# Layer 1 of a two-layer trunk with a routed mixture of experts: another row order for the experts' input weights, and another instruction order on GpSimd

## The chip, the cores and the metric

The kernel runs on one core of a Trainium2 chip. The metric is the device time of one execution in microseconds (us). The kernel before took 2328.43 us (median of 3 runs, 2326.62 to 2334.72). The execution that the profiler recorded took 2327.7 us, and its span, from the first to the last instruction, is 2326.0 us.

The engines are called as in the profile: PE is TensorE (PEld its weight loads), DVE is VectorE, ACT is ScalarE, POOL is GpSimd, SP is SyncE. SP issues nearly all plain loads and stores. POOL issues all indirect transfers (gathers and scatters).

## The reference

Two layers over 1024 tokens of width 1024, float32. Each layer is a mixer (layer 0 a causal pooling mixer, layer 1 gated linear attention, "GLA") and then a mixture of 64 experts, of which every token uses two:

```
for i in range(2):
    shift1, scale1, gate1, shift2, scale2, gate2 = split(silu(c) @ w_mod[i] + b_mod[i], 6)
    h = rmsnorm(x, norm_gain[i, 0]) * (1 + scale1) + shift1
    x = x + gate1 * (pool_mixer(h) if i == 0 else gla_mixer(h))
    h = rmsnorm(x, norm_gain[i, 1]) * (1 + scale2) + shift2
    x = x + gate2 * hier_moe(h)          # group top-1, then two experts of that group
return rmsnorm(x, final_norm_g)

# one expert, over the tokens t routed to it:
gate, up = split(t @ w_in[i, e], 2)      # w_in[i, e] is 1024 x 768
y = (silu(gate) * up) @ w_out[i, e]      # w_out[i, e] is 384 x 1024
```

Each expert's weights are 3 MB (w_in) and 1.5 MB (w_out), read once for each layer whatever the number of its tokens.

## The kernel before

**Weights.** SBUF is divided into 16 slots of [128 partitions, 3072 floats], 1.5 MB each. One expert takes three of them, called thirds: thirds 0 and 1 are the two halves of w_in, third 2 is w_out. `third_load` (L495) issues one 1.5 MB DMA on SP's queue for each. For a half of w_in partition p gets the four rows k*128 + p of that half, which lie apart in memory, 3,072 bytes each. For w_out partition p gets the three rows 3p to 3p+2, 12,288 bytes that lie side by side. In layer 1 the thirds go round a ring of 14 slots (`RING1`), so that loads run up to 14 thirds ahead, and `queued` (L488) makes each load wait until the load three before it has landed (`DEEP` = 3). SP works strictly in order.

**Tokens.** The normalised rows (without scale and shift) lie in HBM as `h_d`. For each expert POOL gathers 64 token rows, as two halves of 512 channels on 128 partitions, into a buffer `XG` (`gather`, L501). `expert_in` (L508) transposes it on PE in four pieces of 128 channels (L512), and applies scale and shift per channel while it moves the pieces from PSUM to SBUF, on ACT (L520) and DVE (L522). The columns of scale and shift are `modA[:, l, 1]` and `sec(l, 3)`, one column of 128 partitions for each block of 128 channels.

**An expert.** `expert_first` multiplies by w_in (L538, 32 matmul instructions on PE), `expert_hidden` makes silu(gate)*up (L545 on ACT, L546 on DVE), `expert_turn` transposes it (L554 on PE, L555 on ACT), `expert_last` multiplies by w_out (L563), and `expert_add` scales the result on DVE (L568) and has POOL add it to the rows of `x_d` by an indirect DMA with accumulation (L569, here called the scatter). One such sequence is called a pass. An expert with more than 64 tokens takes a second pass with the same weights (`expert_either`). Layer 1 has 68 passes for 64 experts. While PE is busy with one expert, the transposes of the next one stand behind its first product (L512 after L538), so that ACT and DVE work beside PE. Each scatter waits until the one before it has landed, since both may add to the same rows.

**Order on POOL in layer 1's mixture.** `moe` (L608) walks over the experts. In the program's text the step of expert e is: `gather` of expert e+4 (L647; `AHEAD1` = 4, eight buffers in `MAIN1`), then `ahead(e + 3)` (a test of the count on L619 and L630, with a gather of the second 64 tokens in it if there are more than 64), then the scatter or scatters of expert e. Four gathers and three tests stand before the loop. The stage is built under

```
    with tc.manual_schedule(engines={ET.PE}):
        moe(1, RING1, MAIN1, (4, 5, 10, 11), load1, AHEAD1, 3)
```

so that PE keeps the program's order, while the scheduler of the framework places the instructions of the other engines, POOL among them. The load of the fourteenth third of the ring has a dependency written by hand on the fourth gather (L1396).

**Before that mixture** the GLA stage of layer 1 runs over 8 tiles of 128 tokens. Its queries, keys, values, gates and residual rows are fetched by indirect gathers on POOL, two tiles ahead (L1138, L1142, L1146, L1147), and in the middle of it the last columns of the modulation are made (`late_mod`, `mod_scale`).

Of the kernel before, what the change touches and what calls it, by code (L numbers as in the profile page):

```python
# [7 lines left out]
F32 = mybir.dt.float32  # L8
# [6 lines left out]
ET = mybir.EngineType  # L15
# [21 lines left out]
def trunk_kernel(ctx, tc, x_in, c_in, norm_gain, w_mod, b_mod, pool_w, pool_b, pool_scale,  # L37
# [4 lines left out]
    V, S, T, G, SP = nc.vector, nc.scalar, nc.tensor, nc.gpsimd, nc.sync  # L42
# [4 lines left out]
    dram = ctx.enter_context(tc.tile_pool(name="dram", bufs=1, space=bass.MemoryType.DRAM))  # L47

    A = [slots.tile([128, 3072], F32, name=f"slot{i}") for i in range(16)]
# [3 lines left out]
    v_d = dram.tile([SEQ, 1024], F32, name="v_d")  # L53
    r_d = dram.tile([SEQ, 1024], F32, name="r_d")
    z_d = dram.tile([SEQ, 16], F32, name="z_d")

    def part(slot, kb, n):
        a = int(kb * 256)
        return A[slot][:, a:a + n]

    def ps():
        return psum.tile([128, 512], F32, name="ps")
# [10 lines left out]
    ident = cv(128)  # L73
# [6 lines left out]
    modA = cv(32).rearrange("p (a b c) -> p a b c", a=2, b=2)  # L80
# [21 lines left out]
    XG = [XGt[:, i, :] for i in range(4)] + [part(15, 7 + 2 * i, 512) for i in range(2)] \  # L102
# [93 lines left out]
    def mod_scale(l, s):  # L196
        V.scalar_tensor_tensor(modA[:, l, s, :], mod[:, l, 24 * s + 8:24 * s + 16], 1.0,
                               C1[:, 96 + (2 * l + s) * 8:96 + (2 * l + s) * 8 + 8], op0=OP.add, op1=OP.mult)

    def sec(l, s):  # L200
        return mod[:, l, 8 * s:8 * s + 8]

    def row(col, half, diag):
        d = diag.rearrange("p (a b) -> p a b", a=4)
# [273 lines left out]
    hv = h_d.rearrange("t (g d) -> (t g) d", g=2)  # L478
    yv = [y.rearrange("t (g d) -> (t g) d", g=2) for y in x_d]

    def expert_load(win, wout, sl):
        behind.clear()
        for j in range(3):
            third_load(win, wout, j, sl)

    behind = []

    def queued(ins):  # L488

        if len(behind) >= DEEP:  # L490
            tc.add_manual_dep(ins.ins, behind[-DEEP].name, DATA_SYNC, reason="loads leave room for gathers")
        behind.append(ins.ins)
        return ins

    def third_load(win, wout, j, sl):  # L495
        if j < 2:
            src = win.rearrange("(k p) f -> p k f", p=128)
            return [queued(SP.dma_start(A[sl[j]].rearrange("p (k f) -> p k f", k=4), src[:, 4 * j:4 * j + 4]))]
        return [queued(SP.dma_start(A[sl[2]], wout.rearrange("(p c) d -> p (c d)", c=3)))]
# [8 lines left out]
    def expert_in(l, i, g, first=None):  # L508
        xT = part(15, 2 * i, 512).rearrange("p (c g t) -> p c g t", c=4, g=2)
        pp = [ps(), ps()]  # L510
        for cc in range(4):
            T.transpose(pp[cc % 2][:, cc // 2 * 128:cc // 2 * 128 + 128], XG[g][:, cc * 128:(cc + 1) * 128], ident)  # L512
        with tc.issue_after(first()) if first else ExitStack():
            for cc in range(4):
                pv = pp[cc % 2][:, cc // 2 * 128:cc // 2 * 128 + 128].rearrange("p (g t) -> p g t", g=2)
                for g in range(2):
                    kc = 4 * g + cc
                    sc, sh = modA[:, l, 1, kc:kc + 1], sec(l, 3)[:, kc:kc + 1]
                    if cc % 2:
                        S.activation(xT[:, cc, g, :], pv[:, g, :], AF.Identity, bias=sh, scale=sc)  # L520
                    else:
                        ins = V.tensor_scalar(xT[:, cc, g, :], pv[:, g, :], sc, sh, op0=OP.mult, op1=OP.add).ins  # L522
        return ins
# [146 lines left out]
    def rest(l, lo, hi, flag, src, sl, bufs):  # L670

        bi, bg = bufs
        base, en = ov[:, 0:1], ov[:, 1:2]
        pb, R, w = ov[:, 2:10], ov[:, 10:34], ov[:, 34:35]
        Rv = R.rearrange("p (t w) -> p t w", w=3)
        Sl = A[sl[0]][:, 0:512]
        nmax = nc.values_load(flag, min_val=0, max_val=SEQ, skip_runtime_bounds_check_because=COUNT_REASON)
        with tc.If(nmax > 128):
            V.memset(en, float(lo))
            with tc.For_i(lo, hi, 1) as e:  # L680
                n = nc.values_load(cnt_i[0:1, bass.ds(e, 1)], min_val=0, max_val=SEQ,
                                   skip_runtime_bounds_check_because=COUNT_REASON)
                with tc.If(n > 128):
                    V.memset(base, 128.0)
                    with tc.For_i(128, n, 64):
                        p = ps()
                        m = 0
                        for k in range(2):
                            V.tensor_scalar(pb, pos(k), base, None, op0=OP.subtract)
                            slots_of(Sl, pb, 0)  # L690
                            V.tensor_scalar(pb, eid(k), en, None, op0=OP.is_equal)
                            for c, a in enumerate((tokno, place, wk(k))):
                                V.tensor_tensor(Rv[:, :, c], pb, a, op=OP.mult)
                            for t in range(NT):
                                for g in range(2):
                                    T.matmul(p[64 * g:64 * g + 64, 0:3], Sl[:, t * 64:(t + 1) * 64], Rv[:, t, :],
                                             start=m == 0, stop=m == 15)
                                m += 1
                        V.tensor_scalar(ovi, p[:, 0:2], 2.0, gcol, op0=OP.mult, op1=OP.add)
                        V.tensor_copy(w, p[:, 2:3])  # L700
                        gather(ovi[:, 0:1], bg)
                        expert_in(l, bi, bg)
                        expert_load(*src(e), sl)
                        expert_out(l, bi, sl, (w, ovi[:, 1:2]), bg)
                        V.tensor_scalar(base, base, 64.0, None, op0=OP.add)
                V.tensor_scalar(en, en, 1.0, None, op0=OP.add)
# [129 lines left out]
    def load0(e, j, sl):  # L836
        r = e // 8
        if r not in regs:
            regs[r] = nc.values_load(cnt_i[0:1, NE + 16 + r:NE + 17 + r], engines=(ET.SP,), min_val=0, max_val=56,
                                     skip_runtime_bounds_check_because="eight times the number of a group")  # L840
        d = bass.ds(regs[r] + e % 8, 1)
        third_load(moe_w_in[0, d].rearrange("o k f -> (o k) f"), moe_w_out[0, d].rearrange("o k f -> (o k) f"), j, sl)

    for s in range(3):
        load0(0, s, RING0[0:3])
# [452 lines left out]
    pulled = [gl_load2(0), gl_load2(1)]  # L1298

    def load1(e, j, sl):  # L1300
        return third_load(moe_w_in[1, e], moe_w_out[1, e], j, sl)

    def fill1(lo, hi):
        for s in range(lo, hi):
# [20 lines left out]
    with tc.manual_schedule(engines={ET.PE}):  # L1325
        for t in range(NT + 2):
# [17 lines left out]
                columns.pop(0)()  # L1344
            if t == 2:
                mod_scale(1, 1)
            if t > 1:
                route_turn(t - 2, 1, xnb, hTb)
            if t > NT:
# [46 lines left out]
    tc.add_manual_dep(load1(4, 1, RING1[12:14] * 2)[0].ins, ins.name, DATA_SYNC,  # L1396
                      reason="what is needed sooner goes first")
    G.memset(part(15, 7, 1024), 0.0)
    with tc.manual_schedule(engines={ET.PE}):
        moe(1, RING1, MAIN1, (4, 5, 10, 11), load1, AHEAD1, 3)  # L1400
    rest(1, 0, NE, cnt_i[0:1, NE + 8:NE + 9],
         lambda e: tuple(w[1, bass.ds(e, 1)].rearrange("o k f -> (o k) f") for w in (moe_w_in, moe_w_out)),
# [44 lines left out]
```

## Time and profile before

| | |
|---|---|
| median of 3 runs | 2328.43 us |
| profiled execution | 2327.7 us |
| its span | 2326.0 us |
| PE busy | 1984.6 us (85%) |
| DVE, ACT, POOL busy | 718.9, 622.7, 496.9 us |
| bytes moved by DMA | 770.03 MB, mean 331 GB/s |
| layer 1's mixture, from expert 0's first matmul to the last one | 1495 to 2295 us of the span |

The page gives busy time per engine, then the span in 40 equal slices of 58 us. A digit is the busy share in tenths. The row DMA is the mean busy share of the 16 DMA engines. For a single stage, the views by window, the waits and the timeline within that stage are of more use than the page.

### The profile page before, as it was taken

How to read it: one execution, taken by the hardware profiler on the slowest of the kernel's cores; microseconds unless marked ns; L12 is line 12 of the kernel's file. 1: busy time of each engine (PE TensorE's matmuls, PEld its weight loads, DVE VectorE, ACT ScalarE, POOL GpSimd, SP SyncE). 2: the span in 40 equal slices, each digit the busy share in tenths (PEclk: the TensorE clock that was granted, in tenths of full speed). 3: DMA queues.
4: the chain of work that ended last, by engine and by line, in shares of the span. 5: the costliest groups of instructions: out<-in, count | busy, mean ns of one | idle time of the engine just before them, and what ended most of it. 6: DMA issues, size and time to landing. Idle time of an engine off the chain costs nothing. (4 is left out here: it accounts for less than half of the span.)

```text
span 2326.0 us, 31279 instructions
## 1 busy us (share of the span) xinstructions
PE 1984.6 (85%) x11195; PEld 945.5 (41%) x11196; DVE 718.9 (31%) x1759; ACT 622.7 (27%) x1418; POOL 496.9 (21%) x422
## 2 busy tenths in 40 slices
PE   7968888899999999999888999888878777778784
PEld 5644333344444444444334565433323332333331
DVE  3454545211121121212147567422211111112122
ACT  4222323322222121212126665221211111112113
POOL 0303222122222221222124110222212212122210
PEclk9979999999999999999988999899999999999997
DMA  9979989998978999989945942699999999999995
GB/s 347 370 297 393 394 292 346 370 342 326 346 286 310 335 363 341 369 313 365 348 132 169 332 165 87 260 395 386 398 382 391 385 380 390 379 391 386 393 382 206
DMA packets 222566, 770.03 MB, mean 331 GB/s; under 512 B 31623, under 2 KB 41261, under 8 KB 201822
## 3 DMA queue, kind: packets, MB, share of 16 engines
q1 hardware_dynamic: 177074, 684.66, 75.4%
q0 software_dynamic: 43856, 77.67, 12.0%
q10 hardware_dynamic: 1372, 4.28, 0.5%
q8 instruction: 154, 2.52, 0.4%
q14 instruction: 110, 0.90, 0.1%
HBM read 735.44 MB, written 69.80 MB: 346 GB/s over the span
## 5 line engine op out<-in xcount | busy, mean ns | idle before, releaser
L538 PE MATMUL ps<-slot,slot 128*64 128x384 f32 x4416 | 757.5, 493 | 94.7 <-DMA slot<-in_moe_w_in_dram 76.2
L538 PEld LDWEIGHTS ps<-slot,slot 128*64 128x64 f32 x4416 | 336.2, 138 | 517.3 <-issue 247.7
L563 PE MATMUL ps<-slot,slot 128*64 128x512 f32 x1656 | 405.4, 626 | 48.0 <-ACT slot L555 46.2
L545 ACT ACTIVATE slot<-ps 64x384 f32<-64x384 f32 x138 | 67.0, 485 | 1265.1 <-PE ps L538 1236.1
L957 PE MATMUL ps<-slot,slot 128*128 128x512 f16 x1152 | 278.8, 388 | 8.6 <-DVEq L1094 5.7
L522 DVE TENSOR_SCALAR slot<-ps,kept 128x64 f32<-128x64 f32 x552 | 151.1, 334 | 339.8 <-PE ps L512 338.5
L546 DVE TENSOR_TENSOR slot<-slot,ps 64x384 f32<-64x384 f32 x138 | 75.8, 549 | 528.4 <-ACT slot L545 527.6
L569 POOL DMA_INDIRECT x_d<-kept x96 | 159.2, 1659 | 362.4 <-DVEq L664 172.1
L563 PEld LDWEIGHTS ps<-slot,slot 128*64 128x64 f32 x1656 | 110.9, 141 | 247.7 <-issue 184.2
L502 POOL DMA_INDIRECT kept<-h_d,kept x96 | 102.1, 1064 | 499.8 <-DMA x_d<-kept 296.6
L520 ACT ACTIVATE slot<-ps,kept 128x64 f32<-128x64 f32 x552 | 178.4, 403 | 59.3 <-PE ps L512 51.2
L568 DVE SCALAR_TENSOR_TENSOR kept<-ps,kept 128x512 f32<-128x512 f32 x96 | 72.0, 750 | 328.8 <-PE ps L563 325.9
L957 PEld LDWEIGHTS <-slot 128*128 128x128 f16 x1152 | 108.2, 100 | 156.3 <-issue 50.1
L554 PE MATMUL ps<-kept,slot 64*128 64x64 f32 x414 | 76.0, 291 | 91.7 <-DVE slot L546 91.4
L554 PEld LDWEIGHTS ps<-kept,slot 64*128 64x128 f32 x414 | 57.8, 202 | 135.7 <-DVE slot L546 102.3
L569 POOL DMA_INDIRECT x_d<-slot,kept x42 | 67.2, 1601 | 159.6 <-DVE slot L568 96.0
L502 POOL DMA_INDIRECT slot<-h_d,kept x42 | 44.2, 1053 | 230.3 <-DMA x_d<-slot,kept 91.5
L1269 PE MATMUL ps<-slot,slot 128*128 128x512 f16 x384 | 85.7, 379 | 1.2 <-DVE slot L1261 0.9
L568 DVE SCALAR_TENSOR_TENSOR slot<-ps,kept 128x512 f32<-128x512 f32 x42 | 31.5, 751 | 122.4 <-PE ps L563 116.5
L512 PE MATMUL ps<-kept 128*128 128x128 f32 x384 | 63.1, 287 | 2.4 <-DMA kept<-h_d,kept 2.4
L512 PEld LDWEIGHTS ps<-kept 128*128 128x128 f32 x384 | 40.4, 141 | 60.5 <-issue 57.1
L1269 PEld LDWEIGHTS <-slot 128*128 128x128 f16 x384 | 37.1, 98 | 46.7 <-issue 2.1
(336 smaller groups left out, 1672.6 us busy)
## 6 DMA issues: line engine op xcount, KB each, us to landing
slot<-in_moe_w_in_dram SPq DMA_DIRECT2D x256, 1536.0 KB, 12.4
slot<-in_moe_w_out_dram SPq DMA_DIRECT2D x128, 1536.0 KB, 13.0
slot<-in_w_mod_dram SPq DMA_DIRECT2D x24, 1536.0 KB, 11.8
slot<-in_gla_w_in_dram SPq DMA_DIRECT2D x8, 1536.0 KB, 8.2
slot<-in_w_mod_dram SPq DMA_DIRECT2D x8, 1152.0 KB, 6.7
h_d<-slot POOLq DMA_DIRECT2D x16, 512.0 KB, 7.1
slot<-in_x_dram SPq DMA_DIRECT2D x8, 512.0 KB, 11.6
slot<-x_d POOLq DMA_DIRECT2D x8, 512.0 KB, 7.2
```

The source lines that it names most:

```text
L502: return G.indirect_dma_start(out=XG[i], out_offset=None, in_=hv, in_offset=bass.IndirectOffsetOnAxis(ap=idx, axis=0), bounds_check=2 * SE ...
L512: T.transpose(pp[cc % 2][:, cc // 2 * 128:cc // 2 * 128 + 128], XG[g][:, cc * 128:(cc + 1) * 128], ident)
L520: S.activation(xT[:, cc, g, :], pv[:, g, :], AF.Identity, bias=sh, scale=sc)
L522: ins = V.tensor_scalar(xT[:, cc, g, :], pv[:, g, :], sc, sh, op0=OP.mult, op1=OP.add).ins
L538: T.matmul(p1[s, 0:384], xT[:, cc, g, :], W[:, u], start=n == 0, stop=n == 7)
L546: return V.tensor_tensor(hh, hh, p1[up, 0:384], op=OP.mult).ins
L554: T.transpose(p3[:, cc * 64:(cc + 1) * 64], hh[:, :, cc], ident[s, s])
L563: T.matmul(p2[g * 64:g * 64 + 64, :], hT[:, cc * 64:(cc + 1) * 64], o[:, cc, g * 512:(g + 1) * 512], start=cc == 0, stop=cc == 2)
L568: V.scalar_tensor_tensor(XG[y], p2, w, G2, op0=OP.mult, op1=OP.mult)
L569: ins = G.indirect_dma_start(out=yv[l], out_offset=bass.IndirectOffsetOnAxis(ap=sidx, axis=0), in_=XG[y], in_offset=None, bounds_check=2 * ...
L957: T.matmul(p, hP[:, m, kc, :], W[:, n, :], start=kc + i == 0, stop=kc == KC - 1 and i == 2)
L1269: T.matmul(p, oT[:, m, kc, :], woh[kc][:, n, half * 512:(half + 1) * 512], start=kc + i == 0, stop=kc == KC - 1 and i == 2)
```

## The change

It has three parts, all for layer 1.

1. A half of layer 1's w_in is loaded with four consecutive rows to a partition: partition p gets rows 4p to 4p+3 of that half, 12,288 bytes side by side. Piece c of the contraction then holds the channels 4p + c, so `expert_in` takes every fourth channel of the gathered rows for its transposes (a step of 16 bytes in the weight operand of PE), and needs scale and shift in that order.
2. `mod_turn` makes those columns once, at tile 3 of the GLA stage: two transposes on PE, one copy on DVE, one DMA into a small HBM tensor `m_d` and two back, all three on POOL's queue. They land in the storage that held layer 0's columns.
3. `ET.Pool` is added to the engines that keep the program's order while `moe` of layer 1 is built.

```diff
+    m_d = dram.tile([2, 8, 128], F32, name="m_d")
...
+    def mod_turn(l, scr):
+        p = ps()
+        T.transpose(p[0:8, 0:128], modA[:, l, 1, :], ident)
+        T.transpose(p[0:8, 128:256], sec(l, 3), ident)
+        V.tensor_copy(scr[0:8, :], p[0:8, 0:256])
+        G.dma_start(m_d.rearrange("v k p -> k v p"), scr[0:8, :].rearrange("k (v p) -> k v p", v=2))
+        for v, a in enumerate((modA[:, 0, 1, :], sec(0, 3))):
+            G.dma_start(a.rearrange("p (g c) -> p g c", g=2), m_d[v].rearrange("(g b) (a c) -> (b a) g c", g=2, c=4))
...
-    def third_load(win, wout, j, sl):
+    def third_load(l, win, wout, j, sl):
+        if j < 2 and l:
+            return [queued(SP.dma_start(A[sl[j]], win.rearrange("(g p k) f -> p g (k f)", g=2, k=4)[:, j]))]
         if j < 2:
             src = win.rearrange("(k p) f -> p k f", p=128)
...
-            T.transpose(pp[cc % 2][:, cc // 2 * 128:cc // 2 * 128 + 128], XG[g][:, cc * 128:(cc + 1) * 128], ident)
+            rows = XG[g].rearrange("p (r c) -> p c r", c=4)[:, cc] if l else XG[g][:, cc * 128:(cc + 1) * 128]
+            T.transpose(pp[cc % 2][:, cc // 2 * 128:cc // 2 * 128 + 128], rows, ident)
...
-                    sc, sh = modA[:, l, 1, kc:kc + 1], sec(l, 3)[:, kc:kc + 1]
+                    sc, sh = modA[:, 0, 1, kc:kc + 1], sec(0, 3)[:, kc:kc + 1]
...
+            if t == 3:
+                mod_turn(1, part(4, 11, 256))
...
-    with tc.manual_schedule(engines={ET.PE}):
+    with tc.manual_schedule(engines={ET.PE, ET.Pool}):
         moe(1, RING1, MAIN1, (4, 5, 10, 11), load1, AHEAD1, 3)
```

How this moves instructions is seen on POOL at two places. The order of PE, ACT and DVE is the same but for the three new instructions and a few branches at the start of the mixture, and SP issues the same loads in the same order.

First place: POOL at the start of layer 1's mixture, before. `kept<-h_d` is a main gather of one of experts 0 to 3; TENSOR_LOAD to the second UNCONDITIONAL_BRANCH is one test of a count with the gather that it guards.

```order
L1398 MEMSET slot_81 128x1024
L502 DMA kept<-h_d,kept 128x512 x2
L619 TENSOR_LOAD kept
L630 COMPARE_AND_BRANCH
L502 DMA slot_81<-h_d,kept 128x512
L630 UNCONDITIONAL_BRANCH
L630 ISA
L630 UNCONDITIONAL_BRANCH
L619 TENSOR_LOAD kept
L630 COMPARE_AND_BRANCH
```

Before, two gathers are followed by four such tests (the first of them is shown whole), and only then by the third and the fourth gather and those of experts 4 to 7.

The same place now (the lines of the file have moved: L517 is the gather, L635 and L646 the test):

```order
L1416 MEMSET slot_81 128x1024
L517 DMA kept<-h_d,kept 128x512 x3
L635 TENSOR_LOAD kept
L646 COMPARE_AND_BRANCH
L517 DMA slot_81<-h_d,kept 128x512
L646 UNCONDITIONAL_BRANCH
L646 ISA
L646 UNCONDITIONAL_BRANCH
L517 DMA kept<-h_d,kept 128x512
L635 TENSOR_LOAD kept
```

Now the fourth gather stands behind one test instead of four. From there on every step reads gather of expert e+4, test of expert e+3, scatter of expert e, where before the gathers ran up to eight experts ahead, each behind the scatter that frees its buffer.

Second place: POOL in the GLA stage, around tile 3, before. The four gathers are those of the residual rows, of queries and keys, of the values and of the gates.

```order
L1147 DMA slot_72<-x_d,kept 128x1024
L1138 DMA slot_74<-qk_d,kept 128x1024
L1142 DMA slot_72<-v_d,kept 128x1024
L1146 DMA slot_80<-r_d,kept 128x1024
L1147 DMA slot_80<-x_d,kept 128x1024
```

And now, with the write of `m_d` (L211) and the two reads (L213):

```order
L1163 DMA slot_72<-x_d,kept 128x1024
L211 DMA m_d<-slot_70 8x2x128
L1154 DMA slot_74<-qk_d,kept 128x1024
L213 DMA kept<-m_d 128x2x4 x2
L1158 DMA slot_72<-v_d,kept 128x1024
L1162 DMA slot_80<-r_d,kept 128x1024
```

The write stands before the gather of queries and keys, and the reads, which wait for the write to land, before the gather of the values.

## Rows read from the trace of the kernel before

**Rows 1.** Slices of the whole span (page, part 2).
```profile
DMA  9979989998978999989945942699999999999995
```

**Rows 2.** By window: length, busy time of each engine, PEclk, DMA share, GB/s.
```profile
1350.00:1400.00 50.00, 50.00 (x342) 31.60 (x340) 33.99 (x83) 34.03 (x60) 6.84 (x9) 1.00 0.42 138
1664.00:2077.00 413.00, 313.02 (x1632) 127.62 (x1629) 76.06 (x193) 65.64 (x192) 86.59 (x66) 0.98 1.02 386
```

**Rows 3.** Waits of PE, 1500 to 2193 us: total, times, longest.
```profile
PE ps L538 <- DMA slot<-in_moe_w_in_dram: 69.5, 60, 3.2
```

**Rows 4.** Waits of SP's queue, 1500 to 2193 us.
```profile
SPq L498 <- DMA slot<-in_moe_w_in_dram: 416.7, 105, 5.9
...
SPq L498 <- DMA kept<-h_d,kept: 20.3, 1, 20.3
SPq L499 <- PE ps L554: 2.7, 8, 0.4
```

**Rows 5.** Timeline of PE: start, length, group, idle before it and what ended that.
```profile
2185.09 2.80 PE L538 MATMUL ps<-slot,slot 128*64 128x384 f32 x16 [1.31 <-DMA slot<-in_moe_w_in_dram]
...
2243.76 5.33 PE L538 MATMUL ps<-slot,slot 128*64 128x384 f32 x32
...
2254.03 5.33 PE L538 MATMUL ps<-slot,slot 128*64 128x384 f32 x32
```

**Rows 6.** Waits of PE, 2193 to 2295 us.
```profile
PE ps L554 <- DVE slot L546: 7.1, 10, 1.2
```

**Rows 7.** DMA, 1529 to 1532.9 us: packets of 3,072 bytes only.
```profile
DMA packets 538, 1.59 MB, mean 407 GB/s; under 512 B 21, under 2 KB 21, under 8 KB 538
q1 hardware_dynamic: 533, 1.59, 103.3%
```

**Rows 8.** DMA, 1511.1 to 1513.6 us: w_out only, 12,288 bytes.
```profile
DMA packets 122, 1.04 MB, mean 418 GB/s; under 512 B 37, under 2 KB 37, under 8 KB 37
```

**Rows 9.** DMA, 56 to 76 us: rows of w_mod, 12,288 bytes.
```profile
DMA packets 775, 8.52 MB, mean 426 GB/s; under 512 B 82, under 2 KB 82, under 8 KB 82
q1 hardware_dynamic: 774, 8.50, 100.8%
```

**Rows 10.** DMA issues, 1503.5 to 2173 us: count, KB each, us to landing.
```profile
slot<-in_moe_w_in_dram SPq DMA_DIRECT2D x105, 1536.0 KB, 12.9
```

**Rows 11.** Timeline, POOL and SP, start of layer 1's mixture.
```profile
1492.59 1.05 POOL L502 DMA_INDIRECT kept<-h_d,kept  x1 [0.30 <-issue]
1499.08 0.99 POOL L502 DMA_INDIRECT kept<-h_d,kept  x1 [5.45 <-DMA h_d<-slot]
1500.38 1.00 POOL L502 DMA_INDIRECT kept<-h_d,kept  x1 [0.30 <-issue]
...
1503.94 0.37 SPq L498 DMA_DIRECT2D slot<-in_moe_w_in_dram  x1
```

**Rows 12.** By window, as in rows 2, start of layer 1's mixture.
```profile
1496.00:1500.00 4.00, 4.00 (x27) 1.72 (x24) 0.00 (x0) 0.12 (x1) 0.92 (x1) 1.00 0.02 4
```

**Rows 13.** Groups by line and form, 1470 to 2300 us: count, busy us, mean ns.
```profile
L554 PEld LDWEIGHTS ps<-kept,slot 64*128 64x128 f32 x204 | 28.5, 202 | 65.4 <-DVE slot L546 65.4
...
L512 PEld LDWEIGHTS ps<-kept 128*128 128x128 f32 x128 | 13.6, 142 | 21.5 <-issue 20.3 <-DMA slot<-h_d,kept 1.2
```

**Rows 14.** Timeline within one pass.
```profile
2229.86 0.56 PE L554 MATMUL ps<-kept,slot 64*128 64x64 f32 x3 [0.59 <-DVE slot L546]
```

**Rows 15.** Timeline of POOL in the GLA stage, around tile 3.
```profile
1346.23 1.07 POOL L1142 DMA_INDIRECT slot<-v_d,kept  x1 [7.59 <-DVE slot L1184]
```

**Rows 16.** DMA issues of the whole run: KB each, median us to landing.
```profile
h_d<-slot POOLq DMA_DIRECT2D x16, 512.0 KB, 7.1
...
z_d<-slot POOLq DMA_DIRECT2D x8, 8.0 KB, 6.3
```

**Rows 17.** DMA issues, 1700 to 2180 us.
```profile
x_d<-kept POOLq DMA_INDIRECT x18, 9.1
```

**Rows 18.** DMA issues, 60 to 90 us.
```profile
h_d<-slot POOLq DMA_DIRECT2D x2, 512.0 KB, 10.0
```

More of the change, by code (lines that the diff above doesn't have):

```diff
@@ L479, in trunk_kernel, with expert_load @@
     yv = [y.rearrange("t (g d) -> (t g) d", g=2) for y in x_d]
-    def expert_load(win, wout, sl):
+    def expert_load(l, win, wout, sl):
         behind.clear()
         for j in range(3):
-            third_load(win, wout, j, sl)
+            third_load(l, win, wout, j, sl)
     behind = []
@@ L702, in rest @@
                         expert_in(l, bi, bg)
-                        expert_load(*src(e), sl)
+                        expert_load(l, *src(e), sl)
                         expert_out(l, bi, sl, (w, ovi[:, 1:2]), bg)
@@ L841, in load0 @@
         d = bass.ds(regs[r] + e % 8, 1)
-        third_load(moe_w_in[0, d].rearrange("o k f -> (o k) f"), moe_w_out[0, d].rearrange("o k f -> (o k) f"), j, sl)
+        third_load(0, moe_w_in[0, d].rearrange("o k f -> (o k) f"), moe_w_out[0, d].rearrange("o k f -> (o k) f"), j, sl)
     for s in range(3):
@@ L1300, in load1 @@
     def load1(e, j, sl):
-        return third_load(moe_w_in[1, e], moe_w_out[1, e], j, sl)
+        return third_load(1, moe_w_in[1, e], moe_w_out[1, e], j, sl)
     def fill1(lo, hi):
```

## The prediction

> **What bounds the kernel now.** The slices of the span come first [rows 1]: the DMA engines are full for most of the run, in every slice but one of the last quarter. The views by window then tell the stages apart [rows 2]. The GLA stage is PE's: PE is busy for 50.00 of 50 us and DMA for 0.42. The long middle of layer 1's mixture is the loads': DMA share 1.02, while PE is busy for 313 of 413 us. The waits say the same from both sides. PE waits for w_in 60 times, 69.5 us in all [rows 3]. SP waits for earlier loads to land, 416.7 us for w_in alone, and hardly for PE to free a slot: 2.7 us [rows 4]. So the stream of loads never stops for PE, and its speed is the stage's speed.
>
> It does not hold to the end. The last time that PE waits for w_in is at 2185 us. After that passes follow each other every 10.27 us (2254.03 less 2243.76) with no wait on a load [rows 5], and the small wait of L554 on DVE, which comes once a pass, counts ten of them [rows 6]. So whatever makes the loads of the stream faster moves PE at 2185 us, and the ten passes behind it, the final norm and the stores move with it. Faster loads after that point give nothing.
>
> **Part 1, w_in in pieces of 12,288 bytes.** The new w_in load has the shape of the w_out load: 128 pieces of 12,288 bytes in place of 512 of 3,072, the same 1.573 MB. The question is what the pieces cost. In a stretch with nothing but the small ones DMA moves 407 GB/s [rows 7], which is 3.865 us for a load. With nothing but the large ones it is 418 GB/s in 2.5 us of this stage [rows 8] and 426 GB/s in 20 us of layer 0 [rows 9], which is 3.763 and 3.692 us. The smallest difference is 0.10 us a load. The largest comes out if the rate is divided by the share that the packets took (407 / 1.033 = 394 and 426 / 1.008 = 422.6): 3.992 less 3.722 is 0.27 us. I take 0.17, from 407 and 426 as they stand, because 20 us is the longest clean stretch.
>
> From the point at which the stream starts, 1503.5 us, to the load that PE waits for at 2185 us, SP issues 105 loads of w_in [rows 10]. 105 x 0.17 = 17.9, with the unrounded 0.173 it is 18.2 us; the ends are 10.5 and 28.4 us. All stay below the 69.5 us that PE waits. Nothing hides this term, since the queue is full. What is late next is PE itself: at 10.27 us a pass it stays below the stream's new period. That was 669.5 us for 52.5 experts, 12.75 us each [rows 10], and becomes 12.40.
>
> The Trainium skill has a smaller price ("DMA: Bandwidth & Descriptors", section "Why small descriptors are slow (HBM only)"): a fixed overhead of about 3 cycles on each packet, with 32 bytes moved in a cycle. By that four small pieces cost 396 cycles and one large piece 387, an estimate of 0.088 us a load and 9.2 us in all, and the kernel would take 2315 us. Rows 7 and 9 show about twice as much.
>
> **Part 1, the transposes.** L512 now reads its weight operand at a step of 16 bytes. L512 loads contiguous weights in 142 ns, and L554, at a step of 12 bytes, in 202 ns [rows 13]. If the new step costs the same 60 ns, four of them add 0.24 us to a pass. Behind L512 PE waits 0.59 us for DVE before it can do L554 [rows 14], and ACT is on its own work till then. So I take 0; the ends are 0 and what the second rival prices.
>
> **Part 2, mod_turn.** Two transposes on PE and a small copy on DVE, in a stage where PE is always busy [rows 2]. A weight load of L512 takes 142 ns [rows 13]; two transposes paced by that come to 0.3 us, and I take that, with 0.6 as the upper end if the DVE copy is on the path too. On POOL the write and the two reads stand ahead of the values' gather, which starts at 1346.23 after POOL had idled 7.59 us [rows 15]. A write of that size (8 KB, z_d) lands in 6.3 us [rows 16], so the reads are issued just within that idle time. If not, the gather is late by a microsecond or two, for a tile that is used a tile later. The columns are first used 150 us later. Cost 0 on POOL.
>
> **Part 3, POOL's order.** The load of the ring's fourteenth third waits for the fourth gather. SP stood 20.3 us at it [rows 4]. The fourth gather was issued at 1500.38, behind four tests that took 5.45 us between the second gather and the third against 0.30 us between plain neighbours: 1.29 us for a test. The load went out at 1503.94 [rows 11], and DMA lay idle before it (share 0.02 [rows 12]). With one test ahead in place of four the gather goes out 3.9 us earlier, at 1496.5, and the load at 1500.0. The stream behind it starts 3.9 us earlier and ends 3.9 us earlier, provided the slots it needs are free. Ends: 0 (PE frees the next slots too late) and 3.9; I take 3.9. From then on gathers run four experts ahead, not eight. Four passes are some 45 us and a gather needs under ten, so 0.
>
> **The sum** is made against the profiled execution, 2327.7 us (0.7 us below the median): 2327.7 - 18.2 - 3.9 + 0.3 = 2305.9, about 2306 us.
>
> **Rivals.**
>
> *No gain in rate.* The stream may be limited by something that does not see the size of the pieces, such as the memory behind it. For it: with the gathers in between, the stage moves 386 GB/s [rows 2], far below either clean stretch, so other things cost too. Against it: the stretches of rows 7 and 9 differ on the same queue. Then only parts 2 and 3 are left: 2327.7 - 3.9 + 0.3 = 2324 us, no change.
>
> *The strided weights show.* The cover is 0.59 us a pass. If each of the four transposes grows by 0.4 us in place of 0.06, a pass grows by 1.0 us, the loads hide that up to 2185 us and the last ten passes do not: 2306 + 10 = 2316 us. The Trainium skill speaks for it ("SBUF — State Buffer", section "Door 1: The DMA port swizzle (why `[64,N]` ≈ `[32,N]`)"): an access that crosses to a new 16-byte line pays a penalty, and a step of 16 bytes crosses each time. The 202 ns of rows 13, at 12 bytes, agree in direction and are small.
>
> *The scatters become the chain (slower).* Each scatter waits for the one before to land, 9.1 us now [rows 17], and in POOL's new order the next gather stands behind it. A packet of a scatter that takes turns with pieces four times as long waits longer. Where all other traffic was 12,288-byte rows, h_d's writes took 10.0 us [rows 18] against 7.1 over the whole run [rows 16]. By that ratio 9.1 becomes 12.8 at worst, and it decides from 12.40, the new period. Up to some 30 us of lag are absorbed, since a gather is issued more than three periods early. It turns slower than before from 13.4 us (52 x 1.0 less 30 gives back the 22 us); at 14 us it is 52 x 1.6 - 30 = 53 us late, 2359 us. Against it: a third of the traffic is large pieces already. The Trainium skill's rule ("DMA: Bandwidth & Descriptors", section "Queues, rings and completion order") is that an engine takes queues in turn, a packet at a time, which is this mechanism; rows 18 and 16 agree with it.
>
> **Chances.** Forecast 0.78; strided weights 0.09; no gain in rate 0.08; scatters 0.05. About 0.3%, 7 us, is what a measurement can tell from no change: below 2321.4 is faster, above 2335.4 slower. The forecast's own ends are 2327.7 - 28.4 - 3.9 = 2295 and 2327.7 - 10.5 + 0.6 = 2318, all faster, and of the strided case most is. No gain in rate is no change, and the scatters are mostly slower. Faster 0.87, same 0.09, slower 0.04. The range, 2296 to 2319 us, holds the forecast and most of the strided case.
>
> **What would show it.** Right: w_in's packets of 12,288 bytes and a clean stretch near 426 GB/s; the period of the loads near 12.4 us; the fourth gather near 1496.5 and the load behind it near 1500; PE's last wait for w_in some 22 us earlier; passes of 10.27 us after it. Wrong: a period still near 12.75, L554's wait for DVE gone and passes longer than 10.3 us, scatters that land after 12 us or more, or PE waiting for gathers (L512 on kept<-h_d). The prediction fails most simply if 3,072-byte pieces cost no more inside the mixed stream than in my two stretches of a few microseconds.

## The result and the profile after

The changed kernel took 2303.32 us (median of 4 runs, 2296.19 to 2306.62) against 2327.52 us before (4 runs): 0.9897 of before, 95% interval 0.9875 to 0.9919. 2306 us was forecast, and faster. The profiled execution took 2305.41 us, its span is 2303.7 us. Lines have moved: L538 is now L554, L512 L528, L554 L570, L563 L579, L568 and L569 L584 and L585, L502 L517, L498 L510 (w_in) and L514 (w_out).

By window, columns as in [rows 2], the long middle of the mixture and the start of it:

```profile
1664.00:2077.00 413.00, 325.90 (x1736) 138.82 (x1734) 79.99 (x205) 67.40 (x204) 90.31 (x69) 1.00 1.01 397
1496.00:1500.00 4.00, 4.00 (x20) 1.59 (x18) 0.00 (x0) 0.00 (x0) 1.00 (x1) 0.74 0.50 153
```

The DMA engines are as full as in [rows 2], but move 397 GB/s for 386, and PE is busy for 326 us of the 413 for 313. At the start, where DMA lay idle [rows 12], it is busy for half of the time. The view of DMA for 1700 to 2180 us:

```profile
DMA packets 25641, 190.12 MB, mean 396 GB/s; under 512 B 7241, under 2 KB 7241, under 8 KB 11015
...
q1 hardware_dynamic: 16383, 178.99, 91.1%
...
x_d<-slot,kept POOLq DMA_INDIRECT x21, 10.1
kept<-h_d,kept POOLq DMA_INDIRECT x20, 10.7
x_d<-kept POOLq DMA_INDIRECT x19, 10.5
```

The loads' queue (q1) now carries 12,288-byte packets. Scatters (`x_d`) land after 10.1 to 10.5 us, 9.1 before [rows 17].

Waits of PE, 1500 to 2193 us, the answer to [rows 3]:

```profile
PE ps L554 <- DMA slot<-in_moe_w_in_dram: 52.5, 58, 2.7
```

Timeline of PE: its last wait for w_in in the stream, and two neighbouring passes behind it, the answer to [rows 5]:

```profile
2157.17 2.80 PE L554 MATMUL ps<-slot,slot 128*64 128x384 f32 x16 [0.99 <-DMA slot<-in_moe_w_in_dram]
...
2219.72 5.33 PE L554 MATMUL ps<-slot,slot 128*64 128x384 f32 x32
...
2226.34 0.56 PE L570 MATMUL ps<-kept,slot 64*128 64x64 f32 x3 [0.62 <-DVE slot L562]
...
2230.00 5.33 PE L554 MATMUL ps<-slot,slot 128*64 128x384 f32 x32
```

That wait comes at 2157 us and not at 2185, the passes behind it come 24 us earlier (2243.76 became 2219.72) and follow each other every 10.28 us as before, and L570 still waits for DVE as in [rows 14]. The weight loads of the transposes, by line and form, the answer to [rows 13]:

```profile
L528 PEld LDWEIGHTS ps<-kept 128*128 128x128 f32 x128 | 17.8, 209 | 20.3 <-issue 20.3
```

They take 209 ns for 142. Timeline of SP and of POOL at the start of the mixture, the answer to [rows 11]:

```profile
1497.29 0.33 SPq L510 DMA_DIRECT2D slot<-in_moe_w_in_dram  x1
1501.25 0.33 SPq L514 DMA_DIRECT2D slot<-in_moe_w_out_dram  x1
```
```profile
1493.90 0.99 POOL L517 DMA_INDIRECT kept<-h_d,kept  x1 [0.30 <-issue]
1497.51 1.00 POOL L517 DMA_INDIRECT slot<-h_d,kept  x1 [2.62 <-DMA h_d<-slot]
```

The fourth gather went out at 1493.90 (before 1500.38), the fourteenth load at 1497.29 (before 1503.94). What SP waits for next, 1480 to 1560 us:

```profile
SPq L510 <- DMA kept<-h_d,kept: 15.0, 1, 15.0
SPq L514 <- PE ps L528: 13.4, 4, 5.3
...
SPq L510 <- PE ps L579: 6.1, 2, 4.9
```

After the gather it is PE, which must free the slots, that holds the loads for some 20 us.

### The profile page after: what moved, and what is told of

Same layout as the page of the kernel before. It is cut to its first block, busy times and chain, and to the rows that moved or that the text cites. A ratio compares the mean times of both kernels' runs of the same rounds, so it can differ in the third digit from the quotient of the medians.

```text
span 2303.7 us, 31289 instructions
## 1 busy us (share of the span) xinstructions
PE 1982.4 (86%) x11197; PEld 952.9 (41%) x11198; DVE 719.3 (31%) x1760; ACT 617.9 (27%) x1418; POOL 498.7 (22%) x425
## 5 line engine op out<-in xcount | busy, mean ns | idle before, releaser
L554 PE MATMUL ps<-slot,slot 128*64 128x384 f32 x4416 | 751.2, 490 | 77.2 <-DMA slot<-in_moe_w_in_dram 57.7
L554 PEld LDWEIGHTS ps<-slot,slot 128*64 128x64 f32 x4416 | 334.9, 137 | 494.9 <-issue 266.7
L579 PE MATMUL ps<-slot,slot 128*64 128x512 f32 x1656 | 403.3, 624 | 50.0 <-ACT slot L571 47.5
L585 POOL DMA_INDIRECT x_d<-kept x96 | 159.4, 1661 | 544.5 <-DVEq L680 172.7
L538 DVE TENSOR_SCALAR slot<-ps,kept 128x64 f32<-128x64 f32 x552 | 151.1, 334 | 339.5 <-PE ps L528 338.1
L579 PEld LDWEIGHTS ps<-slot,slot 128*64 128x64 f32 x1656 | 110.7, 141 | 249.1 <-issue 183.8
L584 DVE SCALAR_TENSOR_TENSOR kept<-ps,kept 128x512 f32<-128x512 f32 x96 | 72.0, 750 | 326.6 <-PE ps L579 323.8
L517 POOL DMA_INDIRECT kept<-h_d,kept x96 | 102.2, 1065 | 307.4 <-DMA x_d<-kept 189.2
L570 PE MATMUL ps<-kept,slot 64*128 64x64 f32 x414 | 75.9, 290 | 85.7 <-DVE slot L562 84.2
L585 POOL DMA_INDIRECT x_d<-slot,kept x42 | 66.9, 1592 | 352.2 <-DVE slot L584 158.3
L570 PEld LDWEIGHTS ps<-kept,slot 64*128 64x128 f32 x414 | 57.9, 202 | 126.3 <-DVE slot L562 93.1
L584 DVE SCALAR_TENSOR_TENSOR slot<-ps,kept 128x512 f32<-128x512 f32 x42 | 31.5, 751 | 124.3 <-PE ps L579 118.3
L528 PEld LDWEIGHTS ps<-kept 128*128 128x128 f32 x384 | 44.6, 163 | 61.4 <-issue 60.8
L528 PE MATMUL ps<-kept 128*128 128x128 f32 x384 | 65.8, 294 | 4.5 <-DMA kept<-h_d,kept 4.5
L571 ACT COPY slot<-ps 128x192 f32<-128x192 f32 x138 | 44.6, 323 | 32.1 <-PE ps L570 32.1
## 6 DMA issues: line engine op xcount, KB each, us to landing
slot<-in_moe_w_out_dram SPq DMA_DIRECT2D x128, 1536.0 KB, 12.8
slot<-in_x_dram SPq DMA_DIRECT2D x8, 512.0 KB, 11.6
```

What stands on the lines that cost most here:

```text
L517: return G.indirect_dma_start(out=XG[i], out_offset=None, in_=hv, in_offset=bass.IndirectOffsetOnAxis(ap=idx, axis=0), bounds_check=2 * SE ...
L554: T.matmul(p1[s, 0:384], xT[:, cc, g, :], W[:, u], start=n == 0, stop=n == 7)
L570: T.transpose(p3[:, cc * 64:(cc + 1) * 64], hh[:, :, cc], ident[s, s])
L579: T.matmul(p2[g * 64:g * 64 + 64, :], hT[:, cc * 64:(cc + 1) * 64], o[:, cc, g * 512:(g + 1) * 512], start=cc == 0, stop=cc == 2)
L584: V.scalar_tensor_tensor(XG[y], p2, w, G2, op0=OP.mult, op1=OP.mult)
L585: ins = G.indirect_dma_start(out=yv[l], out_offset=bass.IndirectOffsetOnAxis(ap=sidx, axis=0), in_=XG[y], in_offset=None, bounds_check=2 * ...
```

## The experiments

The first idea was that of the prediction: the rate of the stream gives most, POOL's order a few microseconds at the start. Twelve kernels were run. Each ratio is to the kernel before on the same chip. "Mixture" is, in the profiled execution, the time from the first product (L554) of layer 1's first pass to that of its last; it leaves out what the earlier stages vary. It comes from one execution for each kernel.

| kernel | ratio to before | median us | mixture us |
|---|---|---|---|
| before | 1 | 2327.52 | 789.7 |
| changed | 0.9897 (0.9875 to 0.9919) | 2303.32 | 767.0 |
| loads only, old order | 1.0085 (1.0055 to 1.0114) | 2349.82 | 807.4 |
| order only | 0.9964 (0.9944 to 0.9984) | 2321.06 | 787.8 |
| changed, small pieces | 0.9978 (0.9960 to 0.9996) | 2323.65 | 790.6 |
| changed, contiguous | 0.9880 (0.9842 to 0.9917) | 2304.25 | 763.6 |
| changed, 6,144 bytes | 0.9917 (0.9892 to 0.9942) | 2314.47 | 774.5 |
| before, 1,536 bytes | 1.0116 (1.0083 to 1.0150) | 2361.09 | 818.2 |
| 6,144 bytes, old order | 0.9944 (0.9922 to 0.9965) | 2320.30 | 777.1 |
| changed, five buffers | 1.0208 (1.0173 to 1.0243) | 2374.88 | 840.6 |
| order only, five buffers | 1.0056 (1.0031 to 1.0080) | 2338.25 | 806.1 |
| changed, no wait | 0.9902 (0.9876 to 0.9929) | 2311.63 | 767.2 |
| changed, layer 0 too | 0.9964 (0.9940 to 0.9988) | 2327.85 | 767.1 |
| changed, order in layer 0 | 0.9928 (0.9902 to 0.9954) | 2310.55 | 765.6 |

**Loads only: the order taken back.**

```diff
-    with tc.manual_schedule(engines={ET.PE, ET.Pool}):
+    with tc.manual_schedule(engines={ET.PE}):
         moe(1, RING1, MAIN1, (4, 5, 10, 11), load1, AHEAD1, 3)
```

> Parts 1 and 2 alone: large pieces, strided transposes and the turned columns, with POOL in the scheduler's order as before. Theory (the rate of the stream gives most): the stream starts at about 1504 us as before, and the loads gain 0.17 to 0.18 us each, about 18 us, so some 2309 to 2310 us against 2327.5. Rival (the new order on POOL gives most of the gain, since it also starts the stream earlier): 2320 us or more.

It is slower than before. The theory missed by 40 us. The rival's "2320 us or more" holds by the letter, but its reason, the earlier start of the stream, is worth 4 to 13 us by the next run and does not explain a loss against the kernel before. The loads are not the cause, since PE waits for them less than before (44.9 us for 69.5). Its longest waits, 2060 to 2250 us, and the longest of them in PE's timeline:

```profile
PE ps L528 <- DMA slot<-h_d,kept: 44.0, 2, 26.1
```
```profile
2066.06 2.80 PE L554 MATMUL ps<-slot,slot 128*64 128x384 f32 x16 [1.66 <-DMA slot<-in_moe_w_in_dram]
2094.91 1.16 PE L528 MATMUL ps<-kept,slot 128*128 128x128 f32 x4 [26.05 <-DMA slot<-h_d,kept]
```

PE stands for 26 us, and once more for 18, at a gather of second tokens. POOL issued it too late, at 2085 us:

```profile
2082.15 1.60 POOL L585 DMA_INDIRECT x_d<-slot,kept  x1 [0.30 <-issue]
2085.00 1.04 POOL L517 DMA_INDIRECT slot<-h_d,kept  x1 [1.24 <-issue]
```

POOL's timeline in this kernel, then in the kernel before, then in the changed one, at the same place (start, length, group, idle before it and what ended that):

```profile
1588.52 1.62 POOL L585 DMA_INDIRECT x_d<-slot,kept  x1 [0.30 <-issue]
1599.88 1.03 POOL L517 DMA_INDIRECT slot<-h_d,kept  x1 [9.74 <-DMA x_d<-slot,kept]
1601.22 1.60 POOL L585 DMA_INDIRECT x_d<-slot,kept  x1 [0.30 <-issue]
```
```profile
1583.63 1.60 POOL L569 DMA_INDIRECT x_d<-slot,kept  x1 [0.31 <-issue]
1593.84 1.03 POOL L502 DMA_INDIRECT slot<-h_d,kept  x1 [8.61 <-DMA x_d<-slot,kept]
1595.18 1.60 POOL L569 DMA_INDIRECT x_d<-kept  x1 [0.30 <-issue]
```
```profile
1596.70 1.60 POOL L585 DMA_INDIRECT x_d<-kept  x1 [7.58 <-DMA x_d<-slot,kept]
1598.94 1.05 POOL L517 DMA_INDIRECT slot<-h_d,kept  x1 [0.64 <-PE ps L570]
1607.02 1.60 POOL L585 DMA_INDIRECT x_d<-kept  x1 [7.03 <-DMA x_d<-kept]
```

This is the new theory. In the scheduler's order the gather of expert e+8 stands behind the scatter of expert e and needs the buffer that this scatter reads, so it waits until the scatter has landed. The next scatter stands behind that gather. POOL's period is the landing plus 1.35 us of gather and gaps: 11.55 us in the rows of before, 12.70 with large pieces. (Landing is here the time from the scatter's start to the next instruction that waits for it; the DMA view's landing is some 0.8 us shorter.) In the new order the gather goes out while the scatter is in flight, and the period is the landing alone, 10.32 us in the rows above. PE's passes take 10.28 us while the ring is full, and then the stream's 12.4 to 12.9 us. Before, POOL falls behind by at most 10 us (issue of a scatter less the start of the next pass's first product) and catches up in the slow passes. With large pieces it is slower than both kinds: between 1550 and 2080 us it takes 12.94 us from scatter to scatter, PE 11.77 us a pass, and the lag grows to 60 us. The gathers of second tokens are tested for only three experts ahead; the one that PE stood at in pass 48 (counted from 0) was issued at 2085 us, behind the scatter of pass 44. In the changed kernel the lag peaks at 14 us. The two waits, 44 us, are about the 40 us of mixture between the two kernels. Whether tests further ahead would save the scheduler's order was not tried.

**Order only.** The kernel before with

```diff
-    with tc.manual_schedule(engines={ET.PE}):
+    with tc.manual_schedule(engines={ET.PE, ET.Pool}):
         moe(1, RING1, MAIN1, (4, 5, 10, 11), load1, AHEAD1, 3)
```

> Part 3 alone: POOL keeps the program's order, everything else as before. Theory: the fourth gather goes out about 6 us earlier and the stream with it, but PE frees the next slots, so 4 to 6 us come out at the end: about 2322 to 2324 us. Rival (order gives most): about 2310 us. Second rival (nothing, since the loads wait for PE's slots anyway): 2327.5 us.

A little more than the theory: 7.7 us less than the median of before on that chip (2328.8), by the interval 4 to 13 us. The profiled span is 4.5 us shorter than that of before, 1.9 of it in the mixture, so the profiles do not settle the size.

**Two orders, three sizes of landing.** The new theory says when the scheduler's order loses: where landing plus gather exceeds the stream's period. Pieces of 6,144 bytes should stay below that.

The load of w_in, with the transposes and columns to match (left out here):

```diff
...
-            return [queued(SP.dma_start(A[sl[j]], win.rearrange("(g p k) f -> p g (k f)", g=2, k=4)[:, j]))]
+            src = win.rearrange("(g a p k) f -> g p a (k f)", g=2, a=2, k=2)
+            return [queued(SP.dma_start(A[sl[j]].rearrange("p (a f) -> p a f", a=2), src[j]))]
...
-    with tc.manual_schedule(engines={ET.PE, ET.Pool}):
+    with tc.manual_schedule(engines={ET.PE}):
```

> Pieces of 6,144 bytes with GpSimd in the scheduler's order (the run with 6,144 bytes, but for the order). Theory (in that order a gather waits for a scatter to land and the next scatter stands behind the gather, so GpSimd's period is the landing plus 1.65 us, and it decides above the stream's period): scatters should land between the 9.1 us of 3,072 bytes and the 10.9 us of 12,288, at about 9.7 us, a period of 11.4 us against a stream of about 12.6; GpSimd keeps up, no long waits of PE for a gather, and the gain of the pieces is kept but for the earlier start: 0.995 of before. Rival (the scheduler's order and larger pieces lose together whatever the landing, half as much with half the change): 1.005 of before.

0.9944, as the theory has it. POOL's timeline there, two steps of gather and scatter:

```profile
1910.14 1.05 POOL L519 DMA_INDIRECT kept<-h_d,kept  x1 [9.14 <-DMA x_d<-kept]
1911.49 1.60 POOL L589 DMA_INDIRECT x_d<-kept  x1 [0.30 <-issue]
1921.05 1.04 POOL L519 DMA_INDIRECT kept<-h_d,kept  x1 [7.96 <-PE ps L558]
1922.40 1.62 POOL L589 DMA_INDIRECT x_d<-kept  x1 [0.30 <-issue]
```

The chain is there with a step of 10.9 us here and a mean of 11.86 from scatter to scatter between 1550 and 2080 us (12.94 in the loads-only kernel). The view gives no landing times for the kernels with 6,144 bytes; a gather that waits for a scatter starts 10.2 us after it in the median, 9.9 before and 11.6 in the loads-only kernel. The stream's passes take 12.7 us, so the lag, which peaks at 17 us, is made up again, and PE has no long wait for a gather.

The opposite test puts the chain into the new order: with five main buffers the gather of e+4 needs the one that scatter e-1 reads. This edit is made to the changed kernel, and to the kernel before with POOL's new order.

```diff
-MAIN1, AHEAD1 = (0, 1, 2, 3, 6, 7, 8, 9), 4
+MAIN1, AHEAD1 = (0, 1, 2, 3, 6), 4
```

> The changed kernel with five main buffers for the gathered rows in place of eight. A gather of expert e+4 then needs the buffer of expert e-1, so it waits until that scatter has landed, and the next scatter stands behind it on GpSimd: the chain scatter, landing, gather, scatter, put into the new order on purpose. Theory (this chain is what made the large pieces lose in the old order): a period of 10.3 us of landing plus 1.7 us for gather and test, 12 us or more in every pass; the passes that now take 10.28 us lose about 2 us each, less what four gathers ahead absorb: 2325 to 2345 us, PE waiting for kept<-h_d. Rival (the scheduler's order lost for another reason, such as the late third and fourth gather or the tests at its start): as the changed kernel, 2303 us.

> The same five buffers with the old row order and POOL in program order (the run with the order alone, but for the buffers). Theory: scatters land after 8.9 us there, so the chain has a period of 10.6 us, below the 12.5 us of the stream of small pieces and only 0.3 us above the passes that are bound by PE: 2321 to 2326 us, within 0.3% of the order alone. Rival (five buffers cost as such, whatever the pieces): as far above the order alone as the large pieces with five buffers are above the changed kernel, 2345 us or more.

With large pieces it lost 3.1% against the changed kernel, more than expected; with small ones 0.9% against the order alone, where nothing was expected. POOL's timeline, large pieces, then PE's largest wait for gathers with large and with small ones (1500 to 2260 us):

```profile
1901.47 1.60 POOL L585 DMA_INDIRECT x_d<-slot,kept  x1 [2.10 <-issue]
1911.83 1.05 POOL L517 DMA_INDIRECT slot<-h_d,kept  x1 [8.76 <-DMA x_d<-slot,kept]
1915.27 1.60 POOL L585 DMA_INDIRECT x_d<-kept  x1 [2.40 <-issue]
```
```profile
PE ps L528 <- DMA kept<-h_d,kept: 62.5, 24, 5.1
```
```profile
PE ps L512 <- DMA kept<-h_d,kept: 48.0, 27, 4.5
```

The expectation put gather and test at 1.7 us. In the rows above they take 3.44: the test of the count stands between gather and scatter, and POOL is idle for 2.40 us there. With it the chain decides for small pieces too (12.89 us from scatter to scatter between 1550 and 2080 us, mean pass 12.03, 806.1 / 67), and by more for large ones (13.38 and 12.55). So the chain is shown as a cause. The pair does not separate the sizes cleanly: with large pieces scatters landed after 9.3 us here, not 10.3, while DMA moved 371 GB/s in place of 396 (1700 to 2180 us). And PE, with its many short stops, also ran at a lower granted clock (0.89 and 0.90 between 1700 and 2000 us, a mean over its levels of 2.4 and 1.2 GHz).

**Size of the pieces.** The 6,144-byte load above in the new order, and, in the kernel before, w_in with the gate and up halves of a row apart (the product then reads each half where it lies, which is left out here):

```diff
...
+            src = win.rearrange("(k p) (u f) -> p u k f", p=128, u=2)
+            return [queued(SP.dma_start(A[sl[j]].rearrange("p (u k f) -> p u k f", u=2, k=4), src[:, :, 4 * j:4 * j + 4]))]
```

> The changed kernel with w_in in pieces of 6,144 bytes (two consecutive rows, 256 pieces a load), transposes and columns to match. Theory (each piece costs a fixed time beside its bytes): 128 pieces against 512 saved 0.18 us a load, so 0.00047 us a piece, and 256 pieces give 0.12 of the 0.18 us: 11.8 of 17.6 us, some 2309 us. Scatters should land between the 9.0 us of small and the 10.3 us of large pieces. Rival (a threshold between 3,072 and 6,144 bytes): the same as the changed kernel, 2303 us; or (a threshold above 6,144): 2321 us as with POOL's order alone.

> The kernel before with w_in of layer 1 in pieces of 1,536 bytes (1,024 pieces a load), the gate half and the up half of a row apart in SBUF. Theory (a fixed time for each piece, 0.00047 us): 0.24 us more a load, 24 us over 100 loads and up to 31 if the whole mixture is then bound by loads: 2352 to 2359 us, scatters landing below 9.0 us. Rival (the size of the pieces matters only above 3,072 bytes, because of rows of memory or the like): 2328 us.

Both came out by the fixed time for each piece. 6,144 bytes gain 0.47% over the order alone, 12,288 bytes 0.67%: seven tenths, where two thirds were expected (13.3 of 20.8 us of the mixture). Each of these ratios is known to some 0.2 to 0.3% only. 1,536 bytes cost 27 us. No threshold is seen. The view of DMA, 1700 to 2180 us, at 6,144 and at 1,536 bytes:

```profile
DMA packets 34846, 188.43 MB, mean 393 GB/s; under 512 B 7119, under 2 KB 7119, under 8 KB 29942
```
```profile
DMA packets 87852, 178.69 MB, mean 372 GB/s; under 512 B 6647, under 2 KB 79799, under 8 KB 83231
```

The records of single packets in these windows say why: their median time is 65, 121, 234 and 460 ns for 1,536, 3,072, 6,144 and 12,288 bytes, that is 8 ns and 0.0368 ns a byte. A load in large pieces has 384 pieces fewer than before, on 16 engines: 384 x 8 / 16 = 0.19 us.

**Strided or contiguous.** First the changed kernel with the old load, then with the old transposes:

```diff
-        if j < 2 and l:
-            return [queued(SP.dma_start(A[sl[j]], win.rearrange("(g p k) f -> p g (k f)", g=2, k=4)[:, j]))]
...
-            rows = XG[g].rearrange("p (r c) -> p c r", c=4)[:, cc] if l else XG[g][:, cc * 128:(cc + 1) * 128]
+            rows = XG[g][:, cc * 128:(cc + 1) * 128]
```

> The changed kernel with the old load of w_in in layer 1 (3,072-byte pieces), so that the rows of the weights do not belong to the transposed channels; strided transposes, turned columns and POOL's new order are all in. Theory (the strided weight loads hide behind DVE, the turned columns cost under 1 us): as with the order alone, about 2323 to 2325 us. Rival (the strided transposes cost on PE): the last ten passes, which are PE's, grow by 0.3 to 1 us each, and the time is 3 to 10 us above that of the order alone.

> The changed kernel with contiguous transposes in layer 1 as before, so that the channels do not belong to the rows of the weights; large pieces, turned columns and POOL's order stay. Theory (L528's 67 ns more a weight load hide in the 0.6 us in which PE waits for DVE): passes of 10.28 us and the same time as the changed kernel, 2303 us, within 2 us. Rival (a part of the stride shows in the PE-bound passes, some 30 of them): 4 x 0.067 x 30 = 8 us faster, 2295 us.

The stride is hidden, as expected. In the traces a pass bound by PE takes 10.28 us with it and 10.27 without; the first pass behind one with second tokens 10.22 and 10.13. Over the 30 passes in question that is about 1 us, below what the ratios tell (0.988 and 0.9897; 0.9978 and 0.9964).

**No wait for the gathers.** The ring's fourteenth load without its dependency on the fourth gather:

```diff
-    tc.add_manual_dep(load1(4, 1, RING1[12:14] * 2)[0].ins, ins.name, DATA_SYNC,
-                      reason="what is needed sooner goes first")
+    load1(4, 1, RING1[12:14] * 2)
```

> The changed kernel without the dependency of the ring's fourteenth load on the fourth gather. Theory (after the fourteenth load the stream waits for PE to free slots, and PE for the gathers): one load goes out some 15 us earlier into an idle queue; at best one load time, 3.7 us, comes out, and if it slows the first gathers by as much, nothing: 2299.5 to 2303 us. Rival (the wait holds back the whole start of the stream): 2294 us or less.

The same as the changed kernel. That load went out before the gathers, and the next one at once ran into PE: SP's longest wait there, 1480 to 1560 us, is

```profile
SPq L514 <- PE ps L528: 25.7, 4, 17.1
```

**The same in layer 0.** First the row order (load, transposes and columns) for layer 0 too, then only POOL's program order there.

```diff
-        if j < 2 and l:
+        if j < 2:
...
-                    sc, sh = modA[:, 0, 1, kc:kc + 1], sec(0, 3)[:, kc:kc + 1]
+                    sc, sh = (modA[:, 0, 1, kc:kc + 1], sec(0, 3)[:, kc:kc + 1]) if l else (modA[:, 0, 0, kc:kc + 1], sec(0, 2)[:, kc:kc + 1])
...
+    mod_turn(0, dg[0][:, 0:256], False)
...
+    mod_read((modA[:, 0, 0, :], sec(0, 2)))
```
```diff
-    with tc.manual_schedule(engines={ET.PE}):
+    with tc.manual_schedule(engines={ET.PE, ET.Pool}):
         moe(0, RING0, (0, 1, 2, 3), (4, 5), load0, 2, 1, filler, before, aside, after)
```

> The changed kernel with the same row order in layer 0 too (large pieces, strided transposes, turned columns read back before the routing). In layer 0 PE is busy for 874 of 960 us and waits for w_in for about 5 us. Theory (faster loads give nothing where PE is the bound, and the strided weight loads hide): 2303 us, from 5 us less to 2 us more. Rival A (the same saving as in layer 1): 2285 us. Rival B (the stride is not hidden on a busy PE): 4 x 0.067 x 70 passes = 19 us slower, 2322 us. Rival C (in layer 0 GpSimd keeps the scheduler's order, and scatters that land later make it the chain, as in the run without the new order): over 2320 us, with PE waiting for gathers.

> The changed kernel with GpSimd in program order in layer 0's mixture as well. Theory (there PE is the bound and waits for a gather for only 3 us): 2298 to 2306 us, the same. Rival (GpSimd also has the spills and fetches of the next stage there, and in program order a scatter that waits for its landing holds them up, until PE waits): 2310 us or more. If it is faster, by the start of layer 0's mixture, it beats both kernels.

Neither beats the changed kernel; the first is 0.67% behind it. Faster loads gain nothing where PE is the bound: from pass 9 to the last of layer 0 the profiled execution falls 5 us further behind the changed one, it does not catch up. That is 0.08 us a pass, not the 0.27 of a stride that shows in full. Kernels with an unchanged layer 0 take 854 to 863 us for the same stretch, and this one 864, so 0.08 us a pass cannot be told from nothing. What it lost came early, 12 us before its first pass and 6 us up to pass 9, with this wait in PE's timeline:

```profile
290.08 1.10 PE L532 MATMUL ps<-kept,slot 128*128 128x128 f32 x4 [9.00 <-DMA slot<-h_d,kept]
```

By its place this is rival C in small, a gather behind scatters that land later. Most of the 12 us at the start need no cause in the edit: kernels with an unchanged layer 0 reach their first pass between 181.3 and 194.7 us, this one at 195.5, and the kernel without the wait, on the same chip, at 191.3. With the order alone in layer 0 the interval overlaps that of the changed kernel; its trace ends layer 0 12.5 us later, which one profile does not settle.

## Why the prediction was right, and where it was not

**The bound** was read rightly: the stream of loads to 2185 us [rows 3, 4], PE after it [rows 5]. All that follows the stream came 24 us earlier.

**The term of the rate** (18.2 us) was right in size. The issue of the first third moved by 6.8 us for expert 7 (1532.76 became 1525.98) and by 24.4 for expert 56 (2168.39 became 2143.96), so 98 loads of w_in gained 17.6 us, 0.18 each, for 0.173 predicted. The period of the loads over these experts fell from 12.97 to 12.61 us; the prediction had 12.75 and 12.40, from another stretch, and the same drop. In the new order large pieces are 0.67%, 15.6 us, faster than the order alone (20.8 us of the mixture in the profiles), and 0.81%, 18.9 us, faster than small pieces with all else as changed (23.6 us). The stretches of [rows 7, 9] were fair ones to take it from. The Trainium skill ("DMA: Bandwidth & Descriptors", section "Why small descriptors are slow (HBM only)") gives about 3 cycles a packet, from which the prediction worked out an estimate of 0.088 us a load. The runs show twice as much: 0.18 us a load, and 8 ns for a packet beside its bytes.

**The term of the start** (3.9 us) came out, though not by its reckoning. The single test before the fourth gather cost no 1.29 us; that gather followed 0.30 us behind the third, and the load went out 6.65 us earlier, some 1 us of that because the earlier stages were done sooner. Then PE held the loads, the end that the prediction put at 0 to 3.9 us. Order alone gave 4 to 13 us by the ratio, but 1.9 us of the mixture in its profile, so the size of this term stays open.

**The step that failed**, without moving the forecast, is the next one of part 3: "From then on gathers run four experts ahead, not eight. Four passes are some 45 us and a gather needs under ten, so 0". Beside large pieces the order is worth 1.9%, some 44 us (1.0085 against 0.9897). The parts do not add: parts 1 and 2 alone give +0.85%, part 3 alone -0.36%, all together -1.03%. The prediction's sum came out because part 3 was in, and in this it was lucky. For the first two parts alone the same sum gives 2310 us, and they make the kernel slower than before.

The mechanism was on the page, as the third rival, but it was hung on the wrong order. The prediction saw that scatters land later beside large pieces (9.1 became 10.1 to 10.9 us; its ratio of [rows 18] to [rows 16] gave 12.8 at worst), and it put the chain into the new order with 12.40 us as the point from which it decides. There POOL goes on some 0.8 us after the DMA view's landing, so a landing of 11.6 us would do. In the old order, where a gather stands between landing and next scatter, 1.35 us less will do, some 10.3 us, and the passes at 10.28 us had already built up a lag. Large pieces took it there: scatters landed after 10.8 to 10.9 us in the loads-only kernel. The sign was in the trace before, in POOL's waits for scatters, 1490 to 2193 us:

```profile
POOL kept L502 <- DMA x_d<-kept: 127.2, 16, 9.4
POOL slot L502 <- DMA x_d<-slot,kept: 91.5, 12, 8.9
```

The prediction looked at POOL only at the start.

**The stride and the columns.** Both at the cost predicted, nearly nothing. A weight load of the transposes grew by 67 ns, not by the 0.4 us of the second rival. The write of `m_d`, its reads and the gather of the values in POOL's timeline, the answer to [rows 15]:

```profile
1335.64 0.64 POOL L211 DMA_DIRECT2D m_d<-slot  x1 [3.09 <-DVE kept L162]
...
1340.17 1.53 POOL L213 DMA_DIRECT2D kept<-m_d  x2 [2.59 <-DMA m_d<-slot]
1345.16 1.13 POOL L1158 DMA_INDIRECT slot<-v_d,kept  x1 [3.46 <-DVE slot L1200]
```

The gather is not held by the reads: its idle time ends with DVE, as before.

## What to carry to other kernels

A change that speeds up one queue should be priced at the transfers of the other queues too: find each chain of the form transfer, landing, next transfer, write down its period, and compare it with the new period of the bound, not the old. Where edits come together, price each with and without the others, since an edit that is worth little alone can be what lets another pay. And a fixed time for each piece, once worked out from the gain between two sizes, gave that of a third and a fourth.

## What was not expected of the hardware

- A 3,072-byte piece costs 121 ns and a 12,288-byte one 460 ns on their engine (medians). By the four sizes, from 1,536 bytes, some 8 ns of each do not depend on the size.
- Gathers on POOL's queue, 2 KB rows, land after 10.7 to 11.1 us beside the large pieces where the scatter is in flight at the same time (the new order), and after 7.5 us where the scatter has landed before them (the old order, large pieces as well; 7.9 in the new order with five buffers, where they wait for it). With small pieces the same step from the old to the new order is 7.3 to 8.1 us.
- The weight load of a 128x128 transpose takes 142 ns contiguous, 208 at a step of 8 bytes (the kernels with 6,144 bytes) and 209 at 16, and that of a 64x128 one 202 at a step of 12: hardly more for the wider step.
- Around PE's stop of 26 us the granted clock was 0.55 (2070 to 2100 us, mostly the level of 1.2 GHz), and the L579 behind it took 5.38 us for 2.79.
